# A delta rule's triangular inverses: three steps of the block recursion on VectorE instead of TensorE

## The chip, the cores and the metric

The kernel runs on one core of one Trainium2 chip. The metric is the device time of one execution, in microseconds (us). An execution of the kernel before takes 1125.41 us (median of 3 runs, 1124.91 to 1126.1). The engines are named as in the profile: PE is the matrix engine (TensorE), PEld its weight loads, DVE is VectorE, ACT is ScalarE, POOL is GpSimd, SP issues most of the transfers.

## The reference

One layer of a decoder trunk is computed for a prompt (16 meta tokens and 512 tokens) and for 8 sample rows of 8 tokens. What the change touches is the gated delta rule of 4 heads, which runs in chunks. Cut to that part:

```python
def gated_delta_chunked(q, k, v, g, beta, state, chunk):
    ...
    gcum = jnp.cumsum(gc, axis=-1)
    decay = jnp.exp(jnp.where(causal, gcum[..., :, None] - gcum[..., None, :], -jnp.inf))
    kb = kc * bc[..., None]
    lower = jnp.where(strict, jnp.einsum('nbhcd,nbhed->nbhce', kb, kc) * decay, 0.0)
    a_mat = lower + jnp.eye(chunk, dtype=jnp.float32)
    rhs = jnp.concatenate([vc * bc[..., None], kb * jnp.exp(gcum)[..., None]], axis=-1)
    sol = lax.linalg.triangular_solve(a_mat, rhs, left_side=True, lower=True, unit_diagonal=True)
    u, w = sol[..., :dv], sol[..., dv:]
    def step(s, xs):
        v_new = u_i - jnp.einsum('bhcd,bhde->bhce', w_i, s)
        ...
```

Around it stand an input projection (1024 x 5640), differential attention over paged keys and values, a convolution and norms ahead of the delta rule, gates, an output projection, and a gated FFN of width 2816.

## The kernel before, in words

All matrices are fp32. A large product is made of three: each weight tile is split into a high part (`whi`, a cast on ACT, L331) and a low part (`wlo`, a subtraction on DVE, L332), the inputs likewise, and PE computes high x high, high x low and low x high. These products write the PSUM tiles `ps_d` and are most of PE's work.

**The delta rule.** `gdn` goes through the four heads. For each head `gdn_chain` works on 4 prompt chunks of 128 rows and on a tail chunk of 80 rows (64 sample rows, 16 meta tokens; `NTL`, chunk number 4). A chunk's matrix is unit lower triangular, and its inverse is built up in blocks:

- `gdn_base` inverts the blocks of 16 on the diagonal. The columns of all five chunks lie side by side in the tile `xc` (128 x 5 x 16). Fourteen steps of three DVE instructions (L1112 a stream shuffle within 32 rows, L1113, L1114) solve them. Then DVE spreads `xc` into block-diagonal matrices: L1124 into `xy[:, :, 0]` (four chunks, 128 x 512), L1118 into `xyt` (tail chunk, 80 x 80). A block of the tail is no longer than 16, so its inverse is complete here.
- `gdn_solve` doubles the blocks, 16 to 32 and 32 to 64 (`LEVELS[128]`). It needs the transposed inverse in folded form, `c`: 128 rows, and for each chunk only the columns of the row's own block. The fold is done on PE: four products of `x` with the constant `fold` (128 x 32 each, into `ps_t`), and a copy on ACT (L1166) into `dd`. Each level is then a product with the masked matrix (`ps_g<-dd,lm`), a copy on ACT (L1173), a product with `x` (`ps_g<-dd,xy`), and a DVE subtraction into `c` (L1181). Between the two levels DVE spreads `c` twice (L1152: into `y` block-diagonal, 128 x 512, and into the folded form for the next level, 128 x 256), PE transposes `y` (four times 128 x 128), and ACT copies the result into `x` (L1191).
- `gdn_solve_tail` runs beside it: PE transposes the tail's matrix (80 x 80), ACT copies it (L1218).
- The last step, 64 to 128, is the end of `gdn_solve`.

**What sets the order.** Work that is to fill PE between the steps of this chain comes from generators: `rest()` (the attention of the samples: transposes `ps_t<-consts,page` of cached pages, scores `ps_s<-KT,qb`, values `ps_s<-page,pT`; then the gates and a branch projection), the next head's projection (`gdn_project`) and this head's gate. `merge` interleaves them. It counts the work of PE that has been issued, in planned us (`self.work`), and a stream that yields a number out of the table `DELAY` is not asked again until so much work of others stands behind it. `DELAY[h][12]` after `gdn_base` is 26, 26, 26 and 19.87; those in the solve are 0.04 to 2.28. The layer that records the program then places the instructions of each engine, so that neighbours in the source need not be neighbours on PE.

Of the kernel before, what the change touches and what calls it, by code (L numbers as in the profile page):

```python
# [13 lines left out]
ALU = mybir.AluOpType  # L14
# [29 lines left out]
NTL = NS + NM  # L44
BASE = 16
LATER = 70
LEVELS = {128: tuple(n for n in (8, 16, 32) if n >= BASE), NTL: tuple(n for n in (8,) if n >= BASE)}
# [4 lines left out]
def _lay_out_constants():  # L52
# [26 lines left out]
    def level(p, q, s):  # L79
        return (p // (2 * s) == q // (2 * s)) & (p % (2 * s) >= s) & (q % (2 * s) < s)  # L80
# [6 lines left out]
    put("fold", i[:, None] % (2 * BASE) == np.arange(2 * BASE)[None, :])  # L87
# [3 lines left out]
    if LEVELS[NTL]:  # L91
        put("levels_t", np.stack([same & level(pos[:, None], pos[None, :], s) for s in LEVELS[NTL]], 1))
# [74 lines left out]
class Body:  # L167
# [679 lines left out]
    def gdn_chain(self, h, st):  # L847
# [110 lines left out]
        yield from self.merge((self.gdn_solve_tail(res), 0.4), (self.gdn_solve(res), 9.0))  # L958
# [114 lines left out]
    def gdn_base(self, kk, q, dec, res):  # L1073
# [36 lines left out]
        for j in range(1, BASE - 1):  # L1110
            r, y = row[:, :, 0 : j + 1], x[:, :, 0 : j + 1]
            nc.vector.stream_shuffle(r, y, [i // BASE * BASE + j for i in range(32)])  # L1112
            nc.vector.tensor_tensor(out=r, in0=r, in1=lc[:, :, j : j + 1].to_broadcast([128, 5, j + 1]), op=ALU.mult)  # L1113
            nc.vector.tensor_tensor(out=y, in0=y, in1=r, op=ALU.subtract)  # L1114
        blocks = self.c("base").rearrange("p (b j) -> p b j", j=BASE)
        xyt = self.t(pool, [n, 2, n], "xyt")
        shape = [n, n // BASE, BASE]
        nc.vector.tensor_tensor(  # L1118
            out=xyt[:, 0].rearrange("p (b j) -> p b j", j=BASE), in0=x[:n, 4].unsqueeze(1).to_broadcast(shape),
            in1=blocks[:n, : n // BASE], op=ALU.mult,  # L1120
        )
        xy = self.t(pool, [128, 4, 2, 128], "xy")
# [5 lines left out]
        res.update(lt=lt, at=at, ltt=ltt, att=att, y=xy, xyt=xyt)  # L1128
        yield DELAY[res["h"]][12]

    def gdn_solve(self, res):
# [34 lines left out]
        nc.scalar.copy(c, cp[:, :, :w])  # L1166
        yield DELAY[res["h"]][13]
        for j, s in enumerate(LEVELS[128]):
            zp = self.ps4("g")[:, :, :w]
            product(zp, lm, c)  # L1170
            k = 64 if j + 1 == nl else 64 * ((nl - 1 - j) % 2) + w
# [19 lines left out]
            nc.scalar.copy(x, tp)  # L1191
# [19 lines left out]

    def gdn_solve_tail(self, res):
        nc, pool = self.nc, self.gpool
        n = NTL
        xy, lt = res["xyt"], res["ltt"]
        tp = self.ps("t")
        self.transpose(tp[:n, :n], xy[:, 0])
        nc.scalar.copy(xy[:, 1], tp[:n, :n])  # L1218
        res.update(yt=xy[:, 1])
        nl = len(LEVELS[n])  # L1220
        if not nl:
            return
        levels = self.c("levels_t", n).rearrange("p (s c) -> p s c", s=nl)
        lm = self.t(pool, [n, nl, n], "lmt")
        nc.gpsimd.tensor_tensor(out=lm, in0=levels, in1=lt.unsqueeze(1).to_broadcast([n, nl, n]), op=ALU.mult)
        yield DELAY[res["h"]][18]
        for j in range(nl):
            last = j == nl - 1
            zp = self.ps("g")
            self.mm(zp[:n, :n], lm[:, j], xy[:, 1], start=True, stop=True)  # L1230
            z = self.t(pool, [n, n], "zt")
            nc.scalar.copy(z, zp[:n, :n])
            yield DELAY[res["h"]][19]
            dp = self.ps("g")[:, : 2 * n].rearrange("p (a t) -> p a t", a=2)
            self.mm(dp[:n, 1], xy[:, 0], z, start=True, stop=True)
            if not last:
                self.mm(dp[:n, 0], z, xy[:, 0], start=True, stop=True)
            s = slice(1, 2) if last else slice(0, 2)
            nc.vector.tensor_tensor(out=xy[:, s], in0=xy[:, s], in1=dp[:n, s], op=ALU.subtract)
            yield DELAY[res["h"]][20]  # L1240

# [1162 lines left out]
```

## Time and profile before

| | |
|---|---|
| time, median of 3 | 1125.41 us |
| span of the profiled execution, first to last instruction | 1122.1 us |
| granted clock of PE, mean | 0.999 |
| PE busy | 1100.6 us (98%) |
| DVE busy | 731.3 us (65%) |
| ACT busy | 524.7 us (47%) |
| POOL busy | 224.9 us (20%) |
| heads of the delta rule | about 225 to 580 us |

The profiled execution has no device time of its own beside its span; the median of the runs is 3.3 us above the span. The busy time of PE counts an instruction from its start to its modelled end; instructions overlap, so that the time that PE gives to one of them is the distance from its start to the next one's start.

### The profile page before, as it was taken

How to read it: one execution, taken by the hardware profiler on the slowest of the kernel's cores; microseconds unless marked ns; L12 is line 12 of the kernel's file. 1: busy time of each engine (PE TensorE's matmuls, PEld its weight loads, DVE VectorE, ACT ScalarE, POOL GpSimd, SP SyncE). 2: the span in 40 equal slices, each digit the busy share in tenths (PEclk: the TensorE clock that was granted, in tenths of full speed). 3: DMA queues.
4: the chain of work that ended last, by engine and by line, in shares of the span. 5: the costliest groups of instructions: out<-in, count | busy, mean ns of one | idle time of the engine just before them, and what ended most of it. 6: DMA issues, size and time to landing. Idle time of an engine off the chain costs nothing.

```text
span 1122.1 us, 22894 instructions
## 1 busy us (share of the span) xinstructions
PE 1100.6 (98%) x8350; PEld 972.3 (87%) x8350; DVE 731.3 (65%) x1893; ACT 524.7 (47%) x1264; POOL 224.9 (20%) x336
## 2 busy tenths in 40 slices
PE   8999999999999999999999999999999999999997
PEld 7887797787787787799999987899999999988886
DVE  6456667695594477575344665599999999752315
ACT  6344444464464465452433244465555555832311
POOL 3231220210110110010000003344445454200000
PEclk9999999999999999999999999999999999999999
DMA  7385426847846856723234354323323332333213
GB/s 204 76 269 167 130 65 201 265 134 253 262 151 217 300 172 226 246 74 76 57 97 131 86 169 138 112 80 87 104 86 104 87 105 76 115 113 103 86 47 122
DMA packets 167354, 156.93 MB, mean 140 GB/s; under 512 B 12307, under 2 KB 123458, under 8 KB 167241
## 3 DMA queue, kind: packets, MB, share of 16 engines
q1 hardware_dynamic: 162833, 147.08, 42.8%
q0 software_dynamic: 3008, 5.16, 1.6%
q10 hardware_dynamic: 1400, 3.22, 0.9%
q8 instruction: 66, 1.08, 0.4%
q14 instruction: 47, 0.39, 0.1%
HBM read 145.54 MB, written 9.88 MB: 139 GB/s over the span
## 4 chain that ended last, share of the span: by engine, by line
PE 81%; DVE 8%; issue 3%; DMA 3%; ACT 2%; POOL 2%; SPq 0%; DVEq 0%; ACTq 0%; POOLq 0%
PE ps_d L289 30%; PE ps_t L289 22%; PE ps_g L289 16%; PE ps_s L289 6%; PE ps_t L437 6%; DVE cy L775 1%; DMA wraw<-in_w_out 1%; PE ps_m L289 1%; POOL grr L401 1%; DVE wlo L332 1%; DMA x<-in_x_prompt 1%; DVE row L1112 0%; ACT KT L1541 0%; DVE row L1113 0%; DVE xc L1114 0%
## 5 line engine op out<-in xcount | busy, mean ns | idle before, releaser
L289 PE MATMUL ps_d<-xhi,whi 128*128 128x256 f32 (+2 forms) x696 | 213.7, 310 | 0.1
L289 PE MATMUL ps_d<-xhi,wlo 128*128 128x256 f32 (+2 forms) x696 | 208.8, 303 | 1.5 <-DVE wlo L332 1.5
L332 DVE TENSOR_TENSOR wlo<-wraw,whi 128x512 fp32r<-128x512 f32 x190 | 143.2, 772 | 101.5 <-ACT whi L331 99.5
L289 PE MATMUL ps_d<-xlo,whi 128*128 128x256 f32 (+2 forms) x696 | 208.0, 302 | 0.0
L331 ACT CAST whi<-wraw 128x512 fp32r<-128x512 f32 x190 | 113.7, 621 | 167.2 <-PE ps_d L289 72.0
L289 PEld LDWEIGHTS ps_d<-xhi,whi 128*128 128x128 f32 x696 | 130.8, 189 | 5.9 <-issue 3.5
L289 PEld LDWEIGHTS ps_d<-xhi,wlo 128*128 128x128 f32 x696 | 130.5, 189 | 3.7 <-DVE wlo L332 2.0
L289 PEld LDWEIGHTS ps_d<-xlo,whi 128*128 128x128 f32 x696 | 131.1, 190 | 2.3 <-issue 2.0
L1541 ACT COPY KT<-ps_t 128x512 f32<-128x512 f32 x106 | 57.3, 601 | 34.3 <-PE ps_t L437 32.3
L332 DVE TENSOR_TENSOR lw<-sw,hw 128x512 fp32r<-128x512 f32 x76 | 69.8, 919 | 5.2 <-ACT hw L331 5.2
L437 PE MATMUL ps_t<-consts,page 128*128 128x128 f32 x512 | 68.1, 279 | 0.8 <-DMA page<-in_cache_k 0.6
L289 PE MATMUL ps_t<-fhit,hw 128*128 128x290 f32 x228 | 68.2, 299 | 0.1
L437 PEld LDWEIGHTS ps_t<-consts,page 128*128 128x128 f32 x512 | 55.6, 140 | 14.2 <-issue 7.8
L289 PE MATMUL ps_t<-fhit,lw 128*128 128x290 f32 x228 | 67.7, 297 | 0.0
L289 PE MATMUL ps_t<-flot,hw 128*128 128x290 f32 x228 | 67.7, 297 | 0.0
L331 ACT CAST hw<-sw 128x512 fp32r<-128x512 f32 x76 | 46.7, 617 | 18.3 <-PE ps_g L289 12.4
L289 PEld LDWEIGHTS ps_t<-fhit,hw 128*128 128x128 f32 x228 | 43.1, 189 | 0.3 <-DVE p L2069 0.3
L289 PEld LDWEIGHTS ps_t<-flot,hw 128*128 128x128 f32 x228 | 43.3, 190 | 0.0
L289 PEld LDWEIGHTS ps_t<-fhit,lw 128*128 128x128 f32 x228 | 43.2, 189 | 0.0
L2044 ACT ACTIVATE fy<-fpre,fw 128x592 f32<-128x592 f32 x22 | 19.5, 885 | 46.4 <-DVE fpre L2004 46.4
L2046 DVE SCALAR_TENSOR_TENSOR fy<-fpre,fw,fy 128x592 f32<-128x592 f32 x44 | 36.5, 830 | 1.0 <-ACT fy L2044 0.4
L289 PE MATMUL ps_s<-KT,qb 128*32 128x256 f32 x512 | 34.0, 385 | 0.6
(722 smaller groups left out, 2861.0 us busy)
## 6 DMA issues: line engine op xcount, KB each, us to landing
page<-in_cache_k SPq DMA_DIRECT2D x128, 256.0 KB, 4.2
page<-in_cache_v SPq DMA_DIRECT2D x128, 256.0 KB, 4.2
wraw<-in_w_in SPq DMA_DIRECT2D x86, 256.0 KB, 3.2
wraw<-in_w_ffn_in SPq DMA_DIRECT2D x50, 256.0 KB, 3.0
wraw<-in_w_down SPq DMA_DIRECT2D x44, 256.0 KB, 2.9
raw<-in_w_ffn_in SPq DMA_DIRECT2D x38, 256.0 KB, 3.0
wraw<-in_w_out SPq DMA_DIRECT2D x16, 256.0 KB, 3.1
x<-in_x_prompt SPq DMA_DIRECT2D x4, 512.0 KB, 7.0
```

Source lines behind the costliest of these rows:

```text
L289: return self.nc.tensor.matmul(out, lhsT, rhs, **kw).ins
L331: self.nc.scalar.copy(hi, raw)
L332: (eng or self.nc.vector).tensor_tensor(out=lo, in0=raw, in1=hi.bitcast(F32), op=ALU.subtract)
L401: nc.gpsimd.tensor_tensor(out=dst, in0=dst, in1=self.mhalf[:rows, :n], op=ALU.pow)
L437: self.nc.tensor.transpose(out, in_, self.ident[:k, :k])
L775: nc.vector.scalar_tensor_tensor(out=y, in0=pre[:, j : j + n], scalar=self.cw[:, ch, 24 + j : 25 + j], in1=y, op0=ALU.mult, op1=ALU.add)
L1541: copy(kt[:, :, 128 * j : 128 * j + 128], tp)
L2044: nc.scalar.activation(y, pre[:, 0:592], AF.Identity, bias=fw[:, m, 19:20], scale=fw[:, m, 16:17])
L2046: nc.vector.scalar_tensor_tensor(out=y, in0=pre[:, j : j + 592], scalar=fw[:, m, 16 + j : 17 + j], in1=y, op0=ALU.mult, op1=ALU.add)
```

## The change

The fold, the transposition between the two levels and the transposition of the tail chunk's inverse go from PE and ACT to DVE, whose transposition works on 32 x 32 blocks.

- In `gdn_base`, DVE multiplies `xc` with the constant `halves16` into a tile of 128 x 160 (five chunks of 32 columns), and one stream transposition turns every block of 32 x 32: the result `cc` is the folded, transposed inverse of all five chunks. The spreading into `xy[:, :, 0]` stays. The tail's transposed inverse `yt` is spread on DVE out of `cc` (80 x 96), in place of `xyt`.
- In `gdn_solve` the four fold products and the copy L1166 are gone; the first level reads `cc`. After the first level DVE spreads `c` into the folded form, transposes `c` (128 x 128) and spreads the result into `x`. The four transpositions on PE and the copy L1191 are gone, as is the spreading of `c` into `y`. Since `y` is no longer filled there, POOL sets its lower left part (64 x 4 x 64) to zero in `gdn_base`.
- `gdn_solve_tail` is gone, and with it a `merge`; `DELAY[h][13]` and `DELAY[h][18]` to `[20]` are not used any more. The rest of `DELAY` is as it was. The constants shrink from 1651 to 1621 columns.

In all, PE has 36 instructions fewer, ACT 12 fewer, DVE 12 more (8 stream transpositions and 4 multiplications; 4 of 80 x 80 became 80 x 96), POOL 4 more.

```diff
-LEVELS = {128: tuple(n for n in (8, 16, 32) if n >= BASE), NTL: tuple(n for n in (8,) if n >= BASE)}
+LEVELS = {128: (16, 32)}
...
-    put("fold", i[:, None] % (2 * BASE) == np.arange(2 * BASE)[None, :])
+    put("halves16", i[:, None] // BASE % 2 == np.arange(2)[None, :])
...
-        yield from self.merge((self.gdn_solve_tail(res), 0.4), (self.gdn_solve(res), 9.0))
+        yield from self.gdn_solve(res)
...
+        xw = self.t(pool, [128, 5, 2, BASE], "row")
+        shape = [128, 5, 2, BASE]
+        nc.vector.tensor_tensor(
+            out=xw, in0=x.unsqueeze(2).to_broadcast(shape),
+            in1=self.c("halves16").unsqueeze(1).unsqueeze(3).to_broadcast(shape), op=ALU.mult,
+        )
+        c = self.t(pool, [128, 5, 2 * BASE], "cc")
+        nc.vector.transpose(c.rearrange("p c j -> p (c j)"), xw.rearrange("p c b j -> p (c b j)"))
+        xy = self.t(pool, [128, 4, 2, 128], "xy")
+        nc.gpsimd.memset(xy[64:128, :, 1, 0:64], 0.0)
         blocks = self.c("base").rearrange("p (b j) -> p b j", j=BASE)
-        xyt = self.t(pool, [n, 2, n], "xyt")
-        shape = [n, n // BASE, BASE]
-        nc.vector.tensor_tensor(
-            out=xyt[:, 0].rearrange("p (b j) -> p b j", j=BASE), in0=x[:n, 4].unsqueeze(1).to_broadcast(shape),
-            in1=blocks[:n, : n // BASE], op=ALU.mult,
-        )
...
+        yt = self.t(pool, [n, 96], "yt")
+        shape = [n, 3, 32]
+        nc.vector.tensor_tensor(
+            out=yt.rearrange("p (b j) -> p b j", j=32), in0=c[:n, 4].unsqueeze(1).to_broadcast(shape),
+            in1=self.c("blocks32", n)[:, 0:3].unsqueeze(2).to_broadcast(shape), op=ALU.mult,
+        )
-        res.update(lt=lt, at=at, ltt=ltt, att=att, y=xy, xyt=xyt)
+        res.update(lt=lt, at=at, ltt=ltt, att=att, y=xy, c=c, yt=yt[:, :n])
...
-        fold = self.c("fold")
-        w = 2 * LEVELS[128][0]
-        cp = self.ps4("t")
-        for i in range(4):
-            self.mm(cp[:, i, :w], x[:, i], fold, start=True, stop=True)
+        c, w = res["c"][:, 0:4], 2 * BASE
         dd = self.t(pool, C4, "dd")
-        c = dd[:, :, 0:w] if nl % 2 else dd[:, :, 64 : 64 + w]
-        nc.scalar.copy(c, cp[:, :, :w])
-        yield DELAY[res["h"]][13]
...
             nc.vector.tensor_tensor(out=c, in0=c, in1=dp, op=ALU.subtract)
-            spread(nc.vector, y, c, f"blocks{w}", 128 // w, w)
-            k = 64 * ((nl - 2 - j) % 2)
-            c2 = dd[:, :, k : k + 2 * w]
+            c2 = dd[:, :, 0 : 2 * w]
             spread(nc.vector, c2, c, f"halves{w}", 2, w)
+            ct = self.t(pool, [128, 5, w], "row")[:, 0:4]
+            nc.vector.transpose(ct.rearrange("p c j -> p (c j)"), c.rearrange("p c j -> p (c j)"))
+            spread(nc.vector, x, ct, f"blocks{w}", 128 // w, w)
             c, w = c2, 2 * w
             yield DELAY[res["h"]][15]
-            tp = self.ps4("t")
-            for i in range(4):
-                self.transpose(tp[:, i], y[:, i])
-            nc.scalar.copy(x, tp)
...
-    def gdn_solve_tail(self, res):
-        ...
```

The order of the instructions, place by place. Numbers behind names tell buffers apart; `consts` is the tile of constants, `lm` the masked matrix of a level, `dd` the scratch tile of the solve.

**PE at the beginning of the fourth head's solve.** Before, and then with the change:

```order
L289 MATMUL ps_d_7744<-xhi_7_85,wlo_7738 128x256
L437 MATMUL ps_t_7757<-consts_66,xyt_7523 80x80
L289 MATMUL ps_t_7762<-consts_66,xy_7525 128x32 x4
L289 MATMUL ps_d_7744<-xhi_7_85,whi_7737 128x256
L289 MATMUL ps_d_7744<-xlo_8_86,whi_7737 128x256
```

```order
L287 MATMUL ps_d_7725<-xhi_7_85,wlo_7719 128x256
L287 MATMUL ps_g_7741<-cc_7501,lm_7738 128x32 x4
L287 MATMUL ps_d_7725<-xhi_7_85,whi_7718 128x256
L287 MATMUL ps_d_7725<-xlo_8_86,whi_7718 128x256
L287 MATMUL ps_d_7725<-xhi_7_85,wlo_7722 128x256
```

The tail's transposition and the fold are gone, and the first level's product stands where they stood; before, it came 12 products of `ps_d` later.

**PE between the two levels of the same head.** Before, and with the change:

```order
L289 MATMUL ps_d_7790<-xhi_9_87,wlo_7741 128x322
L437 MATMUL ps_t_7824<-consts_66,xy_7525 128x128 x4
L289 MATMUL ps_g_7830<-dd_7767,lm_7788 128x64 x4
L289 MATMUL ps_d_7848<-xhi_7_85,whi_7841 128x256
```

```order
L287 MATMUL ps_d_7772<-xhi_9_87,wlo_7719 128x322
L287 MATMUL ps_g_7785<-dd_7740,lm_7747 128x64 x4
L287 MATMUL ps_d_7772<-xhi_9_87,whi_7718 128x322
L287 MATMUL ps_d_7772<-xlo_10_88,whi_7718 128x322
```

The four transpositions are gone, and the second level's product follows the filling work directly.

**DVE at the end of the first head's base and in its solve.** `rc` belongs to the samples' softmax, `z` to the head's gate. Before, and with the change:

```order
L1114 TENSOR_TENSOR xc_3605<-xc_3605,row_3616 128x5x15
L1623 RECIPROCAL rc_3896<-sm_3894 128x1
L1118 TENSOR_TENSOR xyt_3659<-xc_3605,consts_66 80x80
L1124 TENSOR_TENSOR xy_3661<-xc_3605,consts_66 128x4x128
L1624 TENSOR_TENSOR rc_3896<-rc_3896,coef_560 128x1
L844 SCALAR_TENSOR_TENSOR z_883_4388<-z_883_4388,ps_d_4400 128x256
L1181 TENSOR_TENSOR dd_3971<-dd_3971,ps_g_3988 128x4x32
L1152 TENSOR_TENSOR xy_3661<-dd_3971,consts_66 128x4x128
L1152 TENSOR_TENSOR dd_3971<-dd_3971,consts_66 128x4x64
L332 TENSOR_TENSOR wlo_4618<-wraw_4613,whi_4617 128x512
```

```order
L1112 TENSOR_TENSOR xc_3605<-xc_3605,row_3616 128x5x15
L1589 RECIPROCAL rc_3901<-sm_3899 128x1
L1115 TENSOR_TENSOR row_3659<-xc_3605,consts_66 128x160
L1125 TENSOR_TENSOR xy_3663<-xc_3605,consts_66 128x4x128
L1120 STREAM_TRANSPOSE cc_3661<-row_3659 128x160
L1590 TENSOR_TENSOR rc_3901<-rc_3901,coef_560 128x1
L842 SCALAR_TENSOR_TENSOR z_870_4320<-z_870_4320,ps_d_4332 128x256
L1131 TENSOR_TENSOR yt_3666<-cc_3661,consts_66 80x96
L1181 TENSOR_TENSOR cc_3661<-cc_3661,ps_g_3984 128x128
L1159 TENSOR_TENSOR dd_3968<-cc_3661,consts_66 128x4x64
L1185 STREAM_TRANSPOSE row_3991<-cc_3661 128x128
L1159 TENSOR_TENSOR xy_3663<-row_3991,consts_66 128x4x128
```

The transposition that makes `cc` stands behind the large spreading into `xy`; in the solve, the folded form is made ahead of the transposition, and the weight's low part `wlo` has moved behind the solve's instructions.

From the first head's solve on, the filling work lies elsewhere, too: between the first head's solve and the end of the fourth head, products, page transpositions and scores stand in other places of the chain.

More of the change, by code (lines that the diff above doesn't have):

```diff
@@ L90, in _lay_out_constants @@
         put(f"halves{2 * s}", i[:, None] // (2 * s) % 2 == np.arange(2)[None, :])
-    if LEVELS[NTL]:
-        put("levels_t", np.stack([same & level(pos[:, None], pos[None, :], s) for s in LEVELS[NTL]], 1))
     put("blocks_s", (np.arange(NS) // TS)[:, None] == np.arange(NB)[None, :])
@@ L1170, in gdn_solve @@
             product(zp, lm, c)
-            k = 64 if j + 1 == nl else 64 * ((nl - 1 - j) % 2) + w
+            k = 64 if j + 1 == nl else w
             z = dd[:, :, k : k + w]
@@ L1210, in gdn_solve @@
         yield DELAY[res["h"]][17]
-    def gdn_solve_tail(self, res):
[L1213 to L1240, printed above, removed]
     def da_queries(self, pool, first):
```

1 line of the change is left out of this document (removed).

## The prediction

> **What bounds the kernel now.** I read the page's busy times first, then the chain of waits, then a table of stretches, then what PE waited for.
>
> ```profile
> PE 1100.6 (98%) x8350; PEld 972.3 (87%) x8350; DVE 731.3 (65%) x1893; ACT 524.7 (47%) x1264; POOL 224.9 (20%) x336
> PE 81%; DVE 8%; issue 3%; DMA 3%; ACT 2%; POOL 2%; SPq 0%; DVEq 0%; ACTq 0%; POOLq 0%
> ```
>
> The second row is the chain that ended last: PE holds 81% of it, DVE 8%. The share alone doesn't say that PE is full in the stage that changes, so here are stretches (length, then PE, PEld, DVE, ACT, POOL busy, granted clock, transfers):
>
> ```profile
> 0.00:20.00 20.00, 16.98 (x110) 14.19 (x111) 15.03 (x33) 14.68 (x27) 10.78 (x22) 1.00 0.74 217
> 215.00:264.00 49.00, 47.57 (x428) 40.17 (x429) 42.74 (x159) 28.02 (x77) 12.17 (x19) 1.00 0.56 174
> 520.00:548.00 28.00, 28.00 (x248) 27.05 (x247) 7.62 (x15) 10.57 (x29) 0.00 (x0) 1.00 0.27 66
> 588.00:615.00 27.00, 26.08 (x194) 25.84 (x193) 13.40 (x23) 10.15 (x20) 0.00 (x0) 1.00 0.43 126
> 215.00:590.00 375.00, 367.98 (x3299) 312.70 (x3300) 230.93 (x750) 180.40 (x495) 41.05 (x58) 1.00 0.56 173
> ```
>
> 215 to 590 us holds the four heads of the delta rule. PE idles 7.0 us of its 375 (375.00 less 367.98), at full clock, and in the fourth head's solve (520 to 548) not at all. What PE waits for there is short:
>
> ```profile
> PE ps_d L289 <- DVE wlo L332: 1.5, 1, 1.5
> PE ps_t L437 <- DVE on L1054: 1.1, 2, 0.6
> PE ps_t L437 <- DVE kn L930: 0.7, 1, 0.7
> PE ps_t L437 <- DVE xyt L1118: 0.5, 1, 0.5
> ```
>
> So the chain of a head's solve, long as it is, is covered by other work of PE; only once, for 0.5 us, does PE wait for an instruction that the change touches. The time of this stage is the sum of what PE has to do. An instruction taken from PE gives back the time that PE gave to it; one taken from ACT gives nothing; one added to DVE costs only where it makes PE wait.
>
> **What leaves PE.** The price is not the mean duration, since instructions overlap, but the distance from start to start. The fourth head, in the timeline:
>
> ```profile
> 524.00 0.28 PE L289 MATMUL ps_d<-xhi,wlo 128*128 128x256 f32 x1
> 524.11 0.23 PE L437 MATMUL ps_t<-consts,xyt 80*80 80x80 f32 x1
> 524.18 1.02 PE L289 MATMUL ps_t<-consts,xy 128*128 128x32 f32 x8
> 525.03 0.36 PE L289 MATMUL ps_d<-xhi,whi 128*128 128x256 f32 x1
> 525.24 0.28 PE L289 MATMUL ps_d<-xlo,whi 128*128 128x256 f32 x1
> 525.36 0.28 PE L289 MATMUL ps_d<-xhi,wlo 128*128 128x256 f32 x1
> ...
> 531.90 0.60 PE L437 MATMUL ps_t<-consts,xy 128*128 128x128 f32 x4
> 532.34 1.00 PE L289 MATMUL ps_g<-dd,lm 128*128 128x64 f32 x8
> ```
>
> - The fold (the eight records of four products): 525.03 less 524.18, 0.85 us. In the second head (rows below) it is 348.09 less 347.21, 0.88. I take 0.87, four times: 3.5 us.
> - The tail's transposition: 524.18 less 524.11, 0.07 us; with the 0.11 that any product ahead of it takes as its own step, I take 0.1, four times: 0.4 us.
> - The four transpositions between the levels: 532.34 less 531.90, 0.44 us. In the third head they took 0.49 (451.02 less 450.53):
>
> ```profile
> 450.53 0.66 PE L437 MATMUL ps_t<-consts,xy 128*128 128x128 f32 x4
> 451.02 1.00 PE L289 MATMUL ps_g<-dd,lm 128*128 128x64 f32 x8
> ```
>
> I take 0.47, four times: 1.9 us. Together **5.8 us** leave PE. Below, the smaller value of each gives 5.5. Above, the time in which any of these instructions ran, by groups of lines (busy, mean ns of one): 4.5 + 2.6 + 1.0 = 8.1.
>
> ```profile
> L289 PE MATMUL ps_t<-consts,xy 128*128 128x32 f32 x32 | 4.5, 275 | 0.1
> L437 PE MATMUL ps_t<-consts,xy 128*128 128x128 f32 x16 | 2.6, 283 | 0.0
> L437 PE MATMUL ps_t<-consts,xyt 80*80 80x80 f32 x4 | 1.0, 251 | 0.5 <-DVE xyt L1118 0.5
> ```
>
> I choose 5.8, because the neighbours' starts show what was free for others. For a PE transposition the Trainium skill ("TensorE: Matmul & The Clock Gate", Part 4: PE-mode transpose) gives about 275 ns in one kernel, 390 alone; by it the 20 transpositions would be worth 5.5 us and not 2.3. The trace has 0.11 us for each from start to start, and 283 ns only as duration; the measured distance decides.
>
> **Coming back to the filling work.** After the fold, the next two `ps_d` products stand 0.21 us apart (525.03, 525.24) where the following stand 0.12 apart: 0.09 us for each return from an unsplit product to split ones. Counted in the two orders, PE returns in this way 476 times before and 462 times now. 14 times 0.09 is **1.3 us** less. Bounds: nothing, if the step only hides behind the weight load; 1.3.
>
> **What the chain waits for.** DVE gets, per head, a multiplication of 128 x 160, a transposition of 160 columns and one of 128; the tail's spreading stays about as it was. No stream transposition is in the trace. The nearest rows:
>
> ```profile
> L1112 DVE STREAM_SHUFFLE row<-xc 128x25 f32<-128x25 f32 x3 | 0.6, 196 | 0.0
> L1112 DVE STREAM_SHUFFLE row<-xc 128x75 f32<-128x75 f32 x4 | 1.0, 243 | 0.0
> L1113 DVE TENSOR_TENSOR row<-row,lc 128x75 f32<-128x75 f32 x4 | 0.9, 237 | 0.1
> L1152 DVE TENSOR_TENSOR dd<-dd,consts 128x256 f32<-128x256 f32 x4 | 1.7, 418 | 0.0
> L1152 DVE TENSOR_TENSOR xy<-dd,consts 128x512 f32<-128x512 f32 x4 | 2.8, 690 | 0.1
> ```
>
> A shuffle costs (243 - 196) / 50 = 0.94 ns more for each column; 160 columns make 0.32 us, 128 make 0.29. The multiplication lies between the third and fourth row, 0.32. Bounds for one transposition: 0.24 (the shuffle of 75 columns) and 0.69 (the spreading of 512). I take the shuffle's line, since both move data within 32 rows and compute nothing. The Trainium skill ("VectorE: DVE Perf Modes", The three transpose paths) has 311 ns for 128 x 128 in bf16 on VectorE, close to this estimate; its Rules for kernel authors send a 128 x 128 transposition to TensorE, but a 32 x 32 one to DVE, and the blocks here are of 32. DVE has 0.93 us more for each head, 3.7 in all.
>
> The first head, at the end of the base:
>
> ```profile
> 264.69 0.24 DVE L1118 TENSOR_TENSOR xyt<-xc,consts 80x80 f32<-80x80 f32 x1
> 264.85 0.68 DVE L1124 TENSOR_TENSOR xy<-xc,consts 128x512 f32<-128x512 f32 x1
> 265.45 0.15 DVE L1624 TENSOR_TENSOR rc<-rc,coef 128x1 f32<-128x1 f32 x1
> 265.47 0.27 PE L437 MATMUL ps_t<-consts,xyt 80*80 80x80 f32 x1
> 265.58 0.63 PE L289 MATMUL ps_t<-consts,xy 128*128 128x32 f32 x4
> ```
>
> The fold starts at 265.58, when `xy` is done (264.85 + 0.68). With the change the multiplication takes the place of L1118 (starts come 0.08 ahead of the end before), so that `cc` is ready at 264.69 + 0.24 + 0.60 + 0.32 = 265.85. PE, without its two steps, is there at about 265.6 and waits 0.3 us: as long as it does now. The other heads:
>
> ```profile
> 517.85 0.68 DVE L1124 TENSOR_TENSOR xy<-xc,consts 128x512 f32<-128x512 f32 x1
> 442.65 0.27 PE L437 MATMUL ps_t<-consts,xyt 80*80 80x80 f32 x1
> ...
> L1118 DVE TENSOR_TENSOR xyt<-xc,consts x2: 239/239/239, 346.2 to 441.2; 80x80 f32<-80x80 f32 x2
> 343.79 1.07 PE L289 MATMUL ps_s<-KT,qb 128*32 128x256 f32 x16
> 344.79 1.31 PE L437 MATMUL ps_t<-consts,page 128*128 128x128 f32 x10
> 346.61 0.24 PE L437 MATMUL ps_t<-consts,xyt 80*80 80x80 f32 x1 [0.51 <-DVE xyt L1118]
> 347.21 1.05 PE L289 MATMUL ps_t<-consts,xy 128*128 128x32 f32 x8
> 348.09 0.36 PE L289 MATMUL ps_d<-xhi,wlo 128*128 128x256 f32 x1
> ```
>
> In the fourth, `xy` was done at 518.5 and PE came to the solve at 524.1, 5.6 us later. In the third, DVE began `xyt` at 441.2 (the second start of the two in the row of L1118), and PE came at 442.65; `cc` would be there 1.2 us after 441.2. Both cover it. In the second, which had `xyt` at 346.2, PE waited. There, the new order puts 112 page transpositions and 56 scores between the Gram product and the solve, where 96 and 48 stood. At 0.13 us a transposition (1.31 / 10) and 0.125 a score (8 of them from 343.79 to 344.79) PE comes 3.1 us later, and `cc` only 1.2: the wait of **0.5 us** goes. Bounds over the four heads: 0.5 us less; if each transposition takes 0.69 and no cover grows, 4 x (1.2 + 0.4) = 6.4 us more.
>
> ```profile
> L1166 ACT COPY dd<-ps_t 128x128 f32<-128x128 f32 x4 | 1.1, 265 | 7.1 <-PE ps_t L289 7.1
> L1191 ACT COPY xy<-ps_t 128x512 f32<-128x512 f32 x4 | 2.3, 584 | 4.3 <-PE ps_t L437 4.3
> L1218 ACT COPY xyt<-ps_t 80x80 f32<-80x80 f32 x4 | 0.9, 221 | 0.6 <-PE ps_t L437 0.5
> ```
>
> Between the levels the chain gets shorter. Now a spreading of 0.69, one of 0.42, the transpositions on PE and a copy of 0.58 on ACT follow the subtraction; then 0.42 is enough for the next product's operand, and the transposition (0.29) and a spreading (0.69) run while PE multiplies. I cost it at nothing, PE being covered there already. The three copies on ACT (0.27, 0.58, 0.22 us; the first, second and third row) leave an engine that is 47% busy: nothing. POOL's zeros (64 x 256) lie between its 0.11 us for 64 x 16 and 1.0 for `zk`:
>
> ```profile
> L806 POOL MEMSET zk<- x1: 999/999/999, 222.3 to 222.3; 128x1088 f32 x1
> L1101 POOL MEMSET lc<- 64x16 f32 x3 | 0.3, 107 | 24.4 <-DVE row L1113 24.4
> ```
>
> From the second head on they wait for PE's last product with the old `xy`; behind them in POOL's queue stand the issue of the state's transfer, which waits longer (for the state made out of that product), and the root `gf`, for which the wait on `on` above stands. Nothing, then, with up to 0.6 a head if I am wrong.
>
> **The sum.** 5.8 + 1.3 + 0.5 = 7.6 us less PE time. After the heads all products follow PE; in 588 to 615 the loads of the output weights leave PE 0.9 us of idle time, which doesn't grow when both move together. From the span, 1122.1 - 7.6 = 1114.5; the runs lie 3.3 above the span: **1117.8 us**. The moved order I cost at nothing. Its bound on the good side is the idle time of PE in the stage, 7.0 us, of which 0.5 is counted.
>
> **Rivals.**
>
> *Durations.* If PE could not overlap what was removed, each instruction is worth its duration: 32 x 0.275 + 16 x 0.283 + 4 x 0.251 = 14.3 us, and the time is 1125.4 - 14.3 = 1111.1. For it: the 98% busy. Against: the starts.
>
> *Handed back: no change.* `DELAY` stays as it is while the instructions that it spaces are others, and hundreds of PE's rows move. If the first product of every head waits for `cc` (1.2 us, 4 times), and the waits on `on`, `kn` and `wlo` (1.1 + 0.7 + 1.5) come a second time at new places, 8.1 us go back: 1117.8 + 8.1 = 1125.9. For it: the second head's wait shows that the cover can run out. Against: in three heads the cover holds, by the rows above.
>
> *Slower.* DVE becomes what the heads wait for. In 215 to 264 it is busy 42.7 of 49 us, and the new order puts a weight's low part behind the solve's instructions. Weights split late stop PE as they did once, for 1.5 us. If every head loses its 0.93 us of new work on DVE and 1.5 us for weights, with one more 0.9 us for the state's products queued behind, that is 3.3 x 4 = 13.2 us, less 7.6: 1125.4 + 5.6 = 1131.0. It decides from 2.5 us a head. Against: 231 of 375 us for DVE over the four heads, and loads that are split several products ahead.
>
> **How the numbers follow.** The forecast has 0.68 (1114 to 1122.5, by the bounds 5.5 to 8.1, half the idle time, and 4 us of new waits), durations 0.05, handed back 0.16, slower 0.11. A measurement can tell 0.2%, 2.25 us: faster is below 1123.2, slower above 1127.7. Faster: 0.68 + 0.05 + a quarter of handed back, 0.77; slower 0.11; within 0.2% the rest, 0.12. The range that holds 8 in 10 reaches from 1113.5 to 1125: all of the forecast's and the better part of handed back.
>
> **What would show it.** The page after should have about 1093 us of PE busy or somewhat less, 52 records fewer on PE, no `ps_t<-consts,xy` of 128 columns, and stream transpositions of about 0.3 us. PE's idle time in the heads should be 6 to 7 us, with no wait of PE for `cc` above 0.4. The forecast is wrong if the waits of PE for DVE in the heads grow by over 5 us (handed back), if those waits name `wlo` (slower), or if a transposition takes over 0.7 us.

## The result, and the profile after

The change makes the kernel 0.2% slower: 1127.18 us (median of 9 runs, 1126.08 to 1129.57) against 1124.95 for the kernel before (9 runs, 1123.95 to 1126.1), a ratio of 1.0021 with a 95% interval of 1.0012 to 1.0029. Forecast were 1117.8 us and a range that ended at 1125.0, with 0.77 on faster. The loss is just at the 0.2% that the prediction took as the least that can be told.

The page's busy times of the changed kernel, with the shares of its chain of waits (line numbers of the kernels differ by a few: L289 and L437 of before are L287 and L435 here):

```profile
PE 1101.2 (98%) x8298; PEld 968.4 (86%) x8298; DVE 735.8 (65%) x1905; ACT 519.4 (46%) x1252; POOL 221.9 (20%) x340
...
PE 79%; DVE 8%; ACT 4%; DMA 4%; issue 3%; POOL 2%; SPq 0%; DVEq 0%; ACTq 0%; POOLq 0%
```

The 52 records on PE are gone (8298 for 8350), but PE is not less busy (1101.2 for 1100.6), and ACT and transfers have a larger share of the chain (4% each, where 2% and 3% stood).

The new work on VectorE costs what was estimated. Groups of lines of the changed kernel (busy, mean ns of one, idle time before it):

```profile
L1120 DVE STREAM_TRANSPOSE cc<-row 128x160 f32<-128x160 f32 x4 | 1.3, 337 | 0.0
...
L1115 DVE TENSOR_TENSOR row<-xc,consts 128x160 f32<-128x160 f32 x4 | 1.3, 324 | 0.1
...
L1185 DVE STREAM_TRANSPOSE row<-cc 128x128 f32<-128x128 f32 x4 | 1.2, 305 | 0.0
...
L1122 POOL MEMSET xy<- 64x256 f32 x4 | 1.2, 307 | 14.8 <-PE ps_g L287 14.7
```

The multiplication takes 0.324 us, the transpositions 0.337 and 0.305.

To see where the time went, take the stretch from the first product with `gut` (first head) to the first product behind the output weights' split (`bhi`), the same two instructions in every run. The table of stretches of before, then of the changed kernel (length, then PE, PEld, DVE, ACT, POOL busy, granted clock, transfers):

```profile
225.40:630.07 404.67, 396.91 (x3506) 342.64 (x3505) 242.32 (x757) 189.62 (x506) 35.33 (x51) 1.00 0.55 168
```

```profile
226.25:633.86 407.61, 395.46 (x3455) 337.42 (x3453) 246.02 (x768) 184.62 (x494) 33.85 (x55) 1.00 0.55 167
```

The stretch grew by 2.9 us, where 7.6 less were forecast. PE idles 12.15 us in it (407.61 less 395.46) instead of 7.76, and is busy only 1.45 us less. The end moved by 4.1 us in all; 0.85 of that lies in the start-up, ahead of the heads, where nothing was changed. (Between the medians it is 2.2 us, since the profiled execution of before was a short one.)

What PE waited for in the changed kernel, from the view of waits (us in total, times, longest):

```profile
PE ps_s L287 <- DMA page<-in_cache_v: 2.7, 4, 1.4
...
PE ps_t L435 <- DVE on L1052: 1.9, 2, 1.4
PE ps_t L435 <- ACT KT L1507: 1.6, 2, 1.4
PE ps_t L287 <- DVE pT L1561: 1.5, 1, 1.5
PE ps_t L435 <- DVE kn L929: 1.3, 2, 0.9
```

None of these names an instruction that the change added. The view of the tile `cc`, who waited for it (us, times):

```profile
  ACT dd L1173: 9.8, 4
  PEld ps_g L287: 0.5, 2
```

PE's weight loads wait for it 0.5 us in all (that ACT waits only means that it is idle). The three longest waits, in the timeline of the changed kernel (second head, between second and third head, third head):

```profile
320.77 0.65 PE L287 MATMUL ps_g<-kk 128*128 128x128 f32 x4
322.82 0.93 PE L435 MATMUL ps_t<-consts,page 128*128 128x128 f32 x6 [1.40 <-ACT KT L1507]
...
385.26 1.07 PE L287 MATMUL ps_s<-page,pT 128*32 128x256 f32 x16
387.86 0.41 PE L287 MATMUL ps_t<-pT,consts 128*32 128x128 f32 x4 [1.53 <-DVE pT L1561]
...
452.05 0.68 PE L287 MATMUL ps_g<-xy,dbig_low 64*64 64x64 f32 x8
454.10 0.64 PE L287 MATMUL ps_s<-page,pT 128*32 128x256 f32 x8 [1.38 <-DMA page<-in_cache_v]
```

At each of them two pieces of work stand next to each other on PE that now lack something between: page transpositions whose PSUM bank ACT is still emptying (a copy `KT` takes 0.59 us), a transposition that comes right behind the values it depends on, values whose page is still on its way. At the first, ACT was itself held up: ahead of its copies `KT` stands an activation of the convolution that waited for VectorE.

```profile
321.43 0.72 ACT L777 ACTIVATE pre<-cy 128x616 f32<-128x616 f32 x1 [1.39 <-DVE cy L773]
322.06 0.14 ACT L763 COPY tail<-ps_d 128x3 f32<-128x3 f32 x1
322.10 0.18 ACT L764 COPY tail<-ps_d 128x24 f32<-128x24 f32 x1
322.17 1.09 ACT L1507 COPY KT<-ps_t 128x512 f32<-128x512 f32 x2
```

In the kernel before, 24 split products stand on PE at this place (behind the key transpositions, from 318.93 to 322.81); with the change there are two, then page transpositions.

In the kernel before, PE's waits have no row for `KT` or `pT`, and 0.8 us for page values, all of it outside the stretch. Added up by releaser, PE's waits in the stretch went from 6.4 to 6.8 us for VectorE, from 0.3 to 2.5 for ACT, and from none to 1.9 for transfers.

So two readings are open. *Order*: what left PE is worth what was forecast, and the filling work in its new places loses as much and more. *Chain*: the new instructions on VectorE hold PE up. A third, *no worth*: the removed instructions were hidden anyway.

### The profile page after: what moved, and what is told of

Its sections match the earlier page's. It is cut to its first block, busy times and chain, and to the rows that moved or that the text cites. A ratio compares the mean times of both kernels' runs of the same rounds, so it can differ in the third digit from the quotient of the medians.

```text
span 1126.2 us, 22802 instructions
## 1 busy us (share of the span) xinstructions
PE 1101.2 (98%) x8298; PEld 968.4 (86%) x8298; DVE 735.8 (65%) x1905; ACT 519.4 (46%) x1252; POOL 221.9 (20%) x340
## 4 chain that ended last, share of the span: by engine, by line
PE 79%; DVE 8%; ACT 4%; DMA 4%; issue 3%; POOL 2%; SPq 0%; DVEq 0%; ACTq 0%; POOLq 0%
PE ps_d L287 31%; PE ps_t L287 20%; PE ps_g L287 15%; PE ps_s L287 7%; PE ps_t L435 6%; ACT KT L1507 2%; DMA page<-in_cache_v 1%; PE ps_m L287 1%; DVE wlo L330 1%; DMA wraw<-in_w_out 1%; DVE cy L773 1%; DMA x<-in_meta_tokens 1%; DMA wraw<-in_w_ffn_in 1%; POOL grr L399 1%; ACT whi L329 0%
## 5 line engine op out<-in xcount | busy, mean ns | idle before, releaser
L287 PE MATMUL ps_d<-xhi,whi 128*128 128x256 f32 (+2 forms) x696 | 213.6, 310 | 0.5 <-DVE z L842 0.4
L287 PE MATMUL ps_d<-xhi,wlo 128*128 128x256 f32 (+2 forms) x696 | 209.5, 304 | 0.0
L287 PE MATMUL ps_d<-xlo,whi 128*128 128x256 f32 (+2 forms) x696 | 208.2, 302 | 0.0
L287 PEld LDWEIGHTS ps_d<-xhi,whi 128*128 128x128 f32 x696 | 131.4, 190 | 6.0 <-issue 3.5
L287 PEld LDWEIGHTS ps_d<-xlo,whi 128*128 128x128 f32 x696 | 131.6, 190 | 2.4 <-issue 2.2
L287 PEld LDWEIGHTS ps_d<-xhi,wlo 128*128 128x128 f32 x696 | 131.2, 190 | 2.1 <-issue 1.2
L435 PE MATMUL ps_t<-consts,page 128*128 128x128 f32 x512 | 67.6, 279 | 1.7 <-ACT KT L1507 1.4
L435 PEld LDWEIGHTS ps_t<-consts,page 128*128 128x128 f32 x512 | 55.3, 140 | 15.7 <-issue 7.7
L287 PE MATMUL ps_t<-fhit,hw 128*128 128x290 f32 x228 | 67.9, 298 | 0.8 <-DVE p L2035 0.4
L287 PE MATMUL ps_t<-flot,hw 128*128 128x290 f32 x228 | 67.5, 296 | 0.0
L287 PE MATMUL ps_t<-fhit,lw 128*128 128x290 f32 x228 | 67.5, 296 | 0.0
L287 PEld LDWEIGHTS ps_t<-fhit,hw 128*128 128x128 f32 x228 | 43.0, 189 | 1.3 <-DVE p L2035 0.7
L287 PEld LDWEIGHTS ps_t<-flot,hw 128*128 128x128 f32 x228 | 43.2, 189 | 0.0
L287 PEld LDWEIGHTS ps_t<-fhit,lw 128*128 128x128 f32 x228 | 43.0, 189 | 0.0
L287 PE MATMUL ps_s<-KT,qb 128*32 128x256 f32 x512 | 36.1, 385 | 1.1 <-ACT KT L1507 0.3
```

Source lines behind the costliest of these rows:

```text
L287: return self.nc.tensor.matmul(out, lhsT, rhs, **kw).ins
L435: self.nc.tensor.transpose(out, in_, self.ident[:k, :k])
```

## The experiments

Each time is a median, each ratio one to the kernel before, run beside it on the same chip (1124.55 to 1124.92 us there).

### The change in the order of before

The interleaving is given back what it lost with the removed code (a yield, and the planned time of the removed products), so that the program is written in the order of before; and PE is tied row by row to the order of before, by dependencies that set an order and wait for nothing. The table is 450 runs of numbers in the order in which PE's instructions are written.

```diff
-        yield from self.gdn_solve(res)
+        yield from self.merge((self.tail_turn(), 0.4), (self.gdn_solve(res), 9.0))
...
         dd = self.t(pool, C4, "dd")
+        self.work += 4 * 1.68e-3 * w
+        yield DELAY[res["h"]][13]
...
             yield DELAY[res["h"]][15]
+            self.work += 4 * 0.11
...
+    def tail_turn(self):
+        self.work += 0.11
+        return
+        yield
...
+    line = [pe[s + k] for s, n in runs for k in range(n)]
+    for x, y in zip(line, line[1:]):
+        tc.add_manual_dep(y, x.name, kind, reason="PE order")
```

> The change's computation, but PE is held to the order of the kernel before with the 36 removed instructions left out; the other engines follow. Theory 'order' (what leaves PE is worth about 6 us, and the filling work in its new places loses about 10): 5.8 us leave PE, two returns to split products less give 0.2, and the second head now waits for the folded inverse about 0.7 us longer than for the tail's spreading: 1124.95 - 5.3 = 1119.6 us, 1117 to 1121. Rival 'chain' (the new instructions on VectorE themselves make PE wait): within 1.5 us of the change, 1126 to 1128. Rival 'no worth' (what was removed was hidden anyway): as before, 1124 to 1126.

Measured: **1118.65 us**, ratio 0.9946 (0.9933 to 0.9959). The same instructions as in the change, in other places on PE (the other engines follow), are 8.5 us faster than the change and 5.9 faster than before. The change was timed beside other runs of the kernel before; by the two ratios to before (1.0021 and 0.9946) the difference is 8.4 us. 'Chain' and 'no worth' both fall. The page of this kernel, and its stretch between the two landmarks:

```profile
PE 1095.0 (98%) x8298; PEld 966.3 (87%) x8298; DVE 735.2 (66%) x1905; ACT 520.3 (47%) x1252; POOL 227.1 (20%) x340
```

```profile
226.49:625.03 398.54, 390.49 (x3454) 336.86 (x3453) 245.81 (x768) 185.65 (x494) 37.11 (x55) 1.00 0.56 171
```

The stretch is 6.13 us shorter than before and 9.07 shorter than in the change. Worked out from the traces, the distances from each PE record to the next record's start, summed by what the record writes and reads (us; a wait falls to the record ahead of it):

| in the stretch | before | change | held order |
|---|---|---|---|
| `ps_t<-consts,xy` and `xyt` (fold, transpositions; the solve's last step stays) | 7.43 | 1.48 | 1.36 |
| split products of the projections, `ps_d` | 197.65 | 197.72 | 198.67 |
| page transpositions `ps_t<-consts,page` | 41.24 | 42.60 | 40.54 |
| scores `ps_s<-KT,qb` | 23.46 | 23.66 | 23.47 |
| values `ps_s<-page,pT` | 22.94 | 24.74 | 22.94 |
| Gram products `ps_g<-kk` | 4.57 | 6.04 | 4.58 |
| the solve's last step, `ps_g<-xy,dbig_low` | 2.42 | 3.87 | 2.42 |
| all else | 104.96 | 107.50 | 104.56 |
| sum | 404.67 | 407.61 | 398.54 |

The first row is what the change takes from PE: 6.0 us, in the held order and in the change alike. The change pays it back in the rows below (the split products apart). Against the held order 4.1 of the 9.07 us is idle time (12.15 less 8.05), the waits above among it; the other 5.0 are longer steps with no idle interval between them, over many small groups, and no view names one cause for them. Part of them belongs to the waits too, since PE counts as busy up to an instruction's modelled end.

### The two parts apart, in the held order

Only the fold and the tail on VectorE; the transposition between the levels stays as it was:

```diff
             nc.vector.tensor_tensor(out=c, in0=c, in1=dp, op=ALU.subtract)
+            spread(nc.vector, y, c, f"blocks{w}", 128 // w, w)
             c2 = dd[:, :, 0 : 2 * w]
             spread(nc.vector, c2, c, f"halves{w}", 2, w)
-            ct = self.t(pool, [128, 5, w], "row")[:, 0:4]
-            nc.vector.transpose(ct.rearrange("p c j -> p (c j)"), c.rearrange("p c j -> p (c j)"))
-            spread(nc.vector, x, ct, f"blocks{w}", 128 // w, w)
             c, w = c2, 2 * w
             yield DELAY[res["h"]][15]
+            tp = self.ps4("t")
+            for i in range(4):
+                self.transpose(tp[:, i], y[:, i])
+            nc.scalar.copy(x, tp)
```

> Part of the change: the fold and the tail's transposition are on VectorE, the four transpositions between the levels stay on PE with their copy; PE is held to the order of the kernel before without the 20 removed instructions. Theory 'start to start' (each removed instruction is worth the distance to the next one's start): 3.5 + 0.4 = 3.9 us less than before, or 1.9 more than the held order with both parts: 1120.6 us (1119.8 to 1121.3). Rival 'durations': 4.5 + 1.0 us: 1119.1. Rival 'hidden': 1123 to 1125.

Measured: 1121.12 us, ratio 0.9961 (0.9946 to 0.9976), 3.5 us less than before and inside the expected range. The first row of the table falls from 7.43 to 3.37: 4.06 us, forecast 3.9.

Only the transposition between the levels on VectorE; fold, tail and their copies stay (in the kernel before, whose `c` lies in `dd`):

```diff
-            nc.vector.tensor_tensor(out=c, in0=c, in1=dp, op=ALU.subtract)
-            spread(nc.vector, y, c, f"blocks{w}", 128 // w, w)
+            cc = self.t(pool, [128, 4, w], "cc")
+            nc.vector.tensor_tensor(out=cc, in0=c, in1=dp, op=ALU.subtract)
...
-            spread(nc.vector, c2, c, f"halves{w}", 2, w)
+            spread(nc.vector, c2, cc, f"halves{w}", 2, w)
+            ct = self.t(pool, [128, 5, w], "row")[:, 0:4]
+            nc.vector.transpose(ct.rearrange("p c j -> p (c j)"), cc.rearrange("p c j -> p (c j)"))
+            spread(nc.vector, x, ct, f"blocks{w}", 128 // w, w)
...
-            for i in range(4):
-                self.transpose(tp[:, i], y[:, i])
-            nc.scalar.copy(x, tp)
```

> The other part: only the transposition between the levels is on VectorE; fold and tail stay on PE; PE held to the order of before without the 16 removed transpositions. Theory 'start to start': 1.9 us less than before, 1122.7 us (1122 to 1123.4). Rival 'durations': 16 x 0.283 = 4.5 less, 1120.1. Rival 'hidden': 1124 to 1125.

Measured: 1123.93 us, ratio 0.9994 (0.9985 to 1.0003), outside the expected 1122 to 1123.4 and not clear of no change. The row falls from 7.43 to 5.42: 2.01 us, forecast 1.9. But only 0.7 us reaches the end. The view of waits shows where most of the rest went. Before, then this kernel:

```profile
PE ps_t L437 <- DVE on L1054: 1.1, 2, 0.6
...
PE ps_s L289 <- DMA page<-in_cache_v: 0.8, 2, 0.5
```

```profile
PE ps_t L437 <- DVE on L1054: 1.8, 2, 1.1
...
PE ps_s L289 <- DMA page<-in_cache_v: 1.4, 1, 1.4
```

PE comes to the transpositions of `on` and to a page of values sooner, and VectorE and the transfer do not: 0.7 + 0.6 us of the gain is spent waiting. In one fixed order a gain on PE can be used up at the next place that PE does not set. In the first row the two parts add up (4.06 + 2.01 for 6.07), in the time they do not (3.5 + 0.7 for 5.9).

### VectorE's share

The transpositions three times over, in the held order:

```diff
+        for _ in range(3):
             nc.vector.transpose(c.rearrange("p c j -> p (c j)"), xw.rearrange("p c b j -> p (c b j)"))
...
+            for _ in range(3):
                 nc.vector.transpose(ct.rearrange("p c j -> p (c j)"), c.rearrange("p c j -> p (c j)"))
```

> As the held order, but each of the 8 transpositions on VectorE is issued three times (0.34 and 0.31 us each in the profile of the change): 1.28 us more VectorE work in the chain of each head, where the whole change added 0.93 to 0.97. Theory 'order': the chain is covered in the third and fourth head, the first and second may show it between their base and their solve (0.67 us each): 0 to 1.5 us above the held order. Rival 'chain': 1.28 x 4 = 5.1 us above the held order, or more.

Measured: 1120.57 us, ratio 0.9963 (0.9950 to 0.9977), 1.9 more than the held order, for 5.1 us of work put into the chain; the change itself adds 3.9 in the held order (735.2 less 731.3 of DVE busy). The intervals of the two ratios overlap; in the profiles the stretch is 1.55 us longer (400.09 for 398.54). That is a little above the band of 'order' (1.5), far from 'chain', and less than a quarter of the 8.5 us in question. It was tried in the held order alone.

### Which line moved the work

First the held order's kernel without the table: the interleaving as before, PE's order left to the recording layer.

> The change's computation, where the interleaving counts the removed PE work as if it were still issued and keeps the removed yields, so that the order in the source is that of the kernel before; the recording layer is free. The placing by the layer still differs from before in some 8% of the rows (26% in the change). Theory 'order': most of the loss goes, 1118 to 1123 us. Rival 'chain': 1125.5 to 1128, as the change. Rival 'no worth': 1124 to 1126.

Measured: 1122.86 us, ratio 0.9977 (0.9968 to 0.9986). So half of the 8.5 us (4.3) comes from the order in the source, the other half (4.2) from where the layer places instructions. Why it places them otherwise (the chain beside them has other lengths now) is argued and not shown. The first half hangs on one line: with only `yield DELAY[res["h"]][13]` put back, and nothing counted, the program as built has the very same order on all engines as here; and also with 26 and 19.87 in the table raised by its 0.79. Since the order is the same, these two were not timed.

The same line taken out of the kernel before, without and with the uncounted work:

```diff
         nc.scalar.copy(c, cp[:, :, :w])
-        yield DELAY[res["h"]][13]
```

> The kernel before with one line taken out, the yield behind the fold; its work is counted as it was and the tail's stream is merged as it was. If the yield alone is what moved the filling steps (theory 'order', cause narrowed to this line): slow like the version that also left the work uncounted (1142.6 us): 1136 to 1146. If the counted work mattered as well: in between, 1127 to 1136. Rival 'chain': 1124 to 1125.5.

and, besides:

```diff
-        yield from self.merge((self.gdn_solve_tail(res), 0.4), (self.gdn_solve(res), 9.0))
+        w0 = self.work
+        for _ in self.gdn_solve_tail(res):
+            pass
+        self.work = w0
+        yield from self.gdn_solve(res)
...
+        self.work -= 4 * 1.68e-3 * w      # behind the fold's copy
+            self.work -= 4 * 0.11         # behind the transpositions between the levels
```

> The computation of the kernel before (fold, transpositions and copies on PE and ACT), but the interleaving doesn't count that work and doesn't yield behind the fold, as in the change. Theory 'order': the moved filling work costs the kernel before as it cost the change, 1128 to 1136 us. Rival 'chain': no new instruction on VectorE, so as before, 1123.5 to 1126.

Measured: 1133.59 us (ratio 1.0082, 1.0069 to 1.0095) and 1142.58 us (1.0168, 1.0145 to 1.0191). No instruction is added, removed or sized differently, and the kernel before loses 9 and 18 us. 'Chain' expected no difference. The line alone is not as slow as both together, so the first reading of its expectation falls and the second holds: the uncounted work and the dropped merge matter there as well. With both, the loss is larger than was expected (1128 to 1136).

The second of the two kernels met something else. The timeline of its third head, and its stretches there:

```profile
437.72 1.07 PE L289 MATMUL ps_s<-KT,qb 128*32 128x256 f32 x16 [0.78 <-ACT KT L1546]
438.72 0.27 PE L437 MATMUL ps_t<-consts,xyt 80*80 80x80 f32 x1
439.27 1.05 PE L289 MATMUL ps_t<-consts,xy 128*128 128x32 f32 x8 [0.28 <-DVE xy L1128]
440.67 1.40 PE L289 MATMUL ps_g<-dd,lm 128*128 128x32 f32 x6 [0.35 <-ACT dd L1170]
```

```profile
437.40:440.80 3.40, 2.45 (x26) 1.63 (x27) 2.18 (x9) 0.76 (x3) 0.36 (x2) 1.00 0.95 330
440.80:454.40 13.60, 11.64 (x77) 8.05 (x81) 2.09 (x9) 3.57 (x7) 0.00 (x0) 0.50 0.09 24
```

Without filling work the chain's steps stand bare: PE is busy 2.45 of 3.4 us, and then the granted clock is at a half (0.50) for 13.6 us, in which PE is busy 11.64. If that work would have taken half as long at full speed, up to 5.8 us of the 18 are the clock's. The traces nearly bear that out: 16 records of `ps_s<-page,pT` take 1.94 us in this stretch, and 1.07 at full clock in the changed kernel (at 385.26).

### Whether the table fits only its own kernel

The kernel before with 26 and 19.87 raised by 0.79 (its first row, of four alike), and the change with them lowered and raised by 2:

```diff
-        ..., 0.17, 26, 0.79, ...
+        ..., 0.17, 26.79, 0.79, ...
```

> The kernel before, nothing computed differently; only the entries 26 and 19.87 of the table, the planned work that must stand between the base and the solve, are 0.79 larger (as much as the yield that the change dropped), so that filling steps move. Theory 'order' in its strong form (the table fits only its own kernel, any such move costs): 1127 to 1140 us. In its weak form (only the loss of a filling step in the solve costs): 1124 to 1127. Rival 'chain': 1124 to 1125.5.

> The change with the spacing between base and solve 2 smaller (26 becomes 24, 19.87 becomes 17.87). If what was lost is filling work ahead of and in the solve, taking more of it away costs more: above the change's 1127.2 us, 1128 to 1138. If the orders only scatter around the held one, anything from 1119 to 1135.

> The change with that spacing 2 larger (28 and 21.87), more than the 0.79 that gave 1122.9 us (the order in the source of the kernel before). If more filling ahead of the solve is what helps: 1119 to 1123. If only the kernel before's own places are good ones: back up, 1124 to 1132.

Measured: 1131.66 us (1.0063, 1.0048 to 1.0077), 1126.17 (1.0028, 1.0007 to 1.0048) and 1126.22 (1.0011, 1.0002 to 1.0020). For this one move the strong form had it right: the same 0.79 that is worth 4.3 us in the change costs 7.1 in the kernel before. More or less filling ahead of the solve is not what counts, since both moves by 2 end near the change.

### Taking a wait away by hand

In the held order 6 and 7 products that stood behind the transpositions of `on` and of the keys (`kt`) were put ahead of them. On PE, the first place (between first and second head), held order and this kernel:

```diff
 MATMUL ps_d<-xhi_9,wlo 128x336
+MATMUL ps_d<-xhi_9,whi 128x336
+MATMUL ps_d<-xlo_10,whi 128x336
+MATMUL ps_d<-xhi_9,wlo 128x336
+MATMUL ps_d<-xhi_7,whi 128x256
+MATMUL ps_d<-xlo_8,whi 128x256
+MATMUL ps_d<-xhi_7,wlo 128x256
 MATMUL ps_t<-consts,on 128x128
...
 MATMUL ps_t<-consts,kt 128x128
-MATMUL ps_d<-xhi_9,whi 128x336
-MATMUL ps_d<-xlo_10,whi 128x336
-MATMUL ps_d<-xhi_9,wlo 128x336
 MATMUL ps_t<-consts,q 128x128
-MATMUL ps_d<-xhi_7,whi 128x256
-MATMUL ps_d<-xlo_8,whi 128x256
-MATMUL ps_d<-xhi_7,wlo 128x256
```

> As the held order, but at two places (first to second head, third to fourth head) 6 and 7 projection products that stood right behind the transpositions of the previous head's output `on` now stand ahead of them; in the held order PE waits there 0.68 and 1.11 us for VectorE. Theory 'order' (the loss is made of such places, and each can be taken back by moving rows): 0.68 + 1.11 = 1.8 us less than the held order, 1116.9 us (1116 to 1118). Rival: the wait moves on to the next instruction (key transpositions, kn), 1118.2 to 1119.

Measured: 1121.80 us, ratio 0.9978 (0.9968 to 0.9987): 3.2 us slower than the held order, where 'order' had it 1.8 faster and the rival the same. That the wait moves on was right, that it grows was not foreseen. The same place, in the timeline of this kernel:

```profile
305.37 0.70 PE L435 MATMUL ps_t<-consts,on 128*128 128x128 f32 x5
305.90 0.60 PE L435 MATMUL ps_t<-consts,kt 128*128 128x128 f32 x4
308.08 0.33 PE L435 MATMUL ps_t<-consts,q 128*128 128x128 f32 x1 [1.58 <-DVE ob L1066]
```

The wait on `on` is gone there, and one of 1.58 us has come two rows later: the transposition of `q` needs one of the three `ps_t` banks (`on` fills two, its prompt and its tail, `kt` the third), and the bank is free when VectorE has read the transposed `on` out of it (`ob`, L1066). In the held order three products lay between `kt` and `q` as cover; they were among those moved. So the earlier wait covered another one, for the bank. At the second place the wait on `on` fell from 1.11 to 0.28 us, and one of 1.15 us for `ob` came. That the bank is what `q` waits for is read from the releaser and the order of the banks; a fourth bank was not tried. The two places together cost 1.2 us (3.0 of waits for 1.8). The rest of the 3.2 stands further on: in the profiles, among others, PE's waits for `gt` are 1.6 us instead of 0.3, and 1.6 for `gjunk` on ACT are new, while 1.5 for `wlo` are gone; what moved these was not followed.

## Why the prediction was wrong

**What bounds the kernel** was right: PE does. The held order shows it, where 6.1 us less in the stretch became 5.9 us less in the time.

**What leaves PE**, 5.8 us, was right: 6.0 by the trace (7.43 less 1.48, or 1.36 in the held order), 4.06 and 2.01 for the parts that had 3.9 and 1.9. (The smaller values give 5.4 rather than 5.5 as its lower bound; nothing hangs on it.) The rival *durations* (14.3 us) is excluded. With it falls, as a price here, the 275 ns that the Trainium skill ("TensorE: Matmul & The Clock Gate", Part 4: PE-mode transpose) has for a PE transposition in one kernel's context (with bf16): the start-to-start distance decided.

**Coming back to the filling work**, 1.3 us, was not seen: the split products take 197.65 us before and 197.72 with the change, though it returns to them 14 times less. Waits lie in these sums too, so the term is not disproved, but nothing shows it. The held order, with 2 returns fewer, gave 5.9 us without it.

**What the chain waits for** was right in its sizes: transpositions 0.337 and 0.305 us (estimated 0.32 and 0.29), multiplication 0.324 (0.32), 0.5 us of waits of the weight loads for `cc` over all heads, the second head's 0.5 us gone. The Trainium skill's 311 ns for bf16 ("VectorE: DVE Perf Modes", The three transpose paths) agrees with the 305 measured for fp32. POOL's zeros took 0.307 us, inside their bounds, and no row of PE's waits names them.

**The sum** added 3.3 us to the span, the distance of before's profile to the median. In each execution of the later runs the time is 1.8 us above its own span, so 1.5 us of that was only the scatter of one profile.

**The step that failed** is the sentence "The moved order I cost at nothing." Its bound on the good side was written down (7.0 us), the bad side got 4 us inside the forecast's range. The held order prices it: 1127.18 less 1118.65, 8.5 us, more than all that the change gains. The working had the evidence in hand, hundreds of moved rows and a table made for the old chain, and looked for its cost only at the instructions that the change touches.

**Handed back** was the rival that came true in its cause, the table that no longer fits its instructions (half of the loss, by the version with the order in the source as before; the rest is the layer's placing). That its number (1125.9) is near is luck, since its places were others: not `cc` four times and `on`, `kn` and `wlo` once more, but the copies `KT`, page transfers, `pT` and many steps too short to see. The test named for it (waits of PE for VectorE grow by over 5 us) would have missed it, since they grew by 0.4 us in the stretch, those for ACT and transfers by 4.1; PE's busy time, named too (about 1093 us), did tell: 1101.2 in the change, 1095.0 in the held order. **Slower** through VectorE is excluded in the held order by the tripled transpositions; in the change, no row of PE's waits names `wlo`, its sign.

## What to carry to other kernels

A change to an instruction in a planned schedule is two changes, the instruction and the plan; price them apart by holding the bounding engine to the old order before a loss is put down to the instruction. A yield or a delay that belongs to removed code is part of the plan: here one such line was worth 4.3 us in the change, 9 in the kernel before, as much as the work that was removed. The version that beats both kernels is the change in the held order, 1118.65 us; where a table of the whole order is too much, putting back the one yield gives the order that took 1122.86.

## What the runs showed of the hardware that was not expected

The granted clock fell to a half while PE was still at work: in the kernel before with the work uncounted, PE's longest idle interval in the 10 us ahead of the fall was 0.78 us, and it was busy 2.45 us in the last 3.4. In the traces' records of the clock such stretches are 3.41 us long (the change, among others), 6.83 (fold only) or 13.65 (here), those at the very end of the program apart: one, two and four times the same length. The Trainium skill ("TensorE: Matmul & The Clock Gate", Part 1) has a window of about 3.4 us and the same half, and ties the fall to a window in which PE idles; the length agrees, but here PE was at work for over two thirds of it.

One such stretch stands at 47 us in the profile of the change and not in that of before, though the instructions there are the same (stretches of the change, then of before):

```profile
46.00:52.00 6.00, 6.00 (x38) 6.00 (x37) 1.63 (x11) 2.42 (x6) 3.90 (x3) 0.72 0.00 0
```

```profile
46.00:52.00 6.00, 6.00 (x46) 6.00 (x47) 1.59 (x11) 2.41 (x6) 3.90 (x3) 1.00 0.01 3
```

Ahead of it PE had no idle time at all for 3.41 us:

```profile
43.56:46.97 3.41, 3.41 (x41) 2.81 (x33) 1.29 (x6) 0.00 (x0) 0.36 (x2) 1.00 0.31 78
```

So what lets the clock fall is open. The cost can be read: ahead of the stretch the products with `baz` of 336 columns start 0.16 us later than in the profile of before (41.74 for 41.58), and behind it the first `whi` product of 336 columns 1.63 us later (50.61 for 48.98). Part of the scatter from one execution to the next goes with the clock: of the nine executions of the change, the three with a mean granted clock of 0.996 or 0.997 took 1127.95 to 1129.57 us, the other six 1126.08 to 1128.52.
